# A hybrid recurrent and attention layer: other PSUM slots for the output products, staging slots for the first pair, scans emitted later

## The chip, the cores and the metric

The kernel runs on one core of one Trainium2 chip. The metric is the device time of one execution in microseconds (us). The engines are TensorE (PE, whose weight loads are shown apart as PEld), VectorE (DVE), ScalarE (ACT), GpSimd (POOL) and SyncE (SP), which issues the DMA transfers. Each engine works through its own queue in order and waits on semaphores for the others.

## The reference

One layer of a decoder with two groups of heads side by side, for a prompt of 4096 positions and 8 sampled rows:

```python
def rms_norm(x, g):
    xf = x.astype(jnp.float32)
    y = xf * lax.rsqrt(jnp.mean(xf * xf, axis=-1, keepdims=True) + EPS)
    return (y * g.astype(jnp.float32)).astype(x.dtype)

# per layer (DEPTH = 1), D_MODEL = 1024, SEQ = 4096
# xn = rms_norm(x);  proj = xn @ w_in
#   -> RG-LRU input, its gate, q, k, v, attention gate
# RG-LRU group: causal conv of width 4, then h_t = a_t*h_{t-1} + sqrt(1-a_t^2)*(i_t*x_t)
# attention group: window of 128 keys, 8 query heads, 2 key heads, bias, sinks
# mix = concat(groups * SiLU(gate));  y = x + rms_norm(mix @ w_out)
```

The step that matters here is the last line: a product of 4096 x 1024 activations with the 1024 x 1024 matrix w_out, the norm of each row of the result, and the residual.

## The kernel before

Stage A goes through the positions in 11 chunks (the first of 256 + 8 sampled rows, the others of 384): transpose of the input (prep_A), the recurrent projections (proj_A), the maps of the recurrence (rnn_A) and its scan on VectorE (scan_A). The list A_ORDER at line 32 sets the order in which these are written. Stage B does the projections of the attention group and the attention itself, in units named like 10_1; in its units pT is the transposed probabilities, ph their first half, po the product with V. Both leave their gated results, transposed, in DRAM (mix_d).

Stage C, from line 752, multiplies by w_out. It takes row tiles of 128 in 16 pairs. Numbers are kept as the sum of a coarse part h and a rest l (function parts: ACT makes h, DVE makes l), and a product of two such pairs is three matmuls. Pairs 0 to 2 and 15 go through plain (line 835): two outputs of 512 columns for each row tile (three for the last tile: 512, 256 and 256). Pairs 3 to 14 go through seven (line 872): the pair and w_out are taken as 2 x 2 blocks of 512, and seven products x1 to x7 take the place of eight. One product is 12 matmuls of 512 columns, a pair is 84. ACT copies x1 to u1; DVE makes u2 from x6 and u1, u4 from x5 and u2, adds u4 to x3 and u1 to x2 and so ends the first row tile, makes u3 from x7 and u2, adds u4 to x7 and u3 to x4 and so ends the second. For each row tile ACT makes the squares (squares, line 811) while DVE multiplies by the gain, and finish (line 823) scales by the root and adds the residual, in two operations that read both halves of the row tile in PSUM. Names end in the pair: x7_9, h_9s3 and l_9s3 are of pair 9; finish for the second row tile of pair 6 has the root rs_c6b.

PSUM in stages B and C has these pools: ps_mm, two slots of one bank (512 columns); ps_t and ps_v, one slot of one bank each; ps_s, two slots of two banks each. In seven before, x1, x6 and x5 take turns in ps_mm; x2 and x3 are the two halves of one ps_s tile (x23), x4 and x7 of another (x47); ps_t and ps_v stand empty there but for the 8 sampled rows (function sample_rows, 32 small matmuls, written at pair 4). A slot is handed on when all readers of its tile are done.

The activations of a pair are loaded by load_mix (line 760): two transfers of 512 KB into one tile of tag m, of which there are two slots in turn. The tags hl, hs and long hold the operands h and l; each pair is written out a step ahead of its products. In pairs 0 to 2 prep_T also makes the sums of blocks of w_out that seven needs (wt, th, tl). A scheduler of the framework then sets the order of each engine's queue from the written order, the slots and its estimate of durations, so that the order in the queues is not that of the code.

The pools of the staging area are shared by all stages: tag xf has two slots, used in stage A for the small constants and in the last tile for its output.

Of the kernel before, what the change touches and what calls it, by code (L numbers as in the profile page):

```python
# [9 lines left out]
F32 = mybir.dt.float32  # L10
# [5 lines left out]
P = 128  # L16
# [12 lines left out]

A_ORDER = "P1 L P0 P2 R1 X0 R0 P3 X1 R2 X2 R3 S X3".split()

B_FIRST = "V Q0 K Q1 U00 U01 Q2 Q3 G0 U02 U10 G1 U11 U12 M00 M01 G2 G3 M02 X M10 M11 M12".split()
B_ORDER = "Q0 Q1 K Q2 V U00 U01 Q3 U02 U10 G0 U11 G2 G1 M00 M01 M02 U12 G3 M10 M11 M12 X".split()
# [9 lines left out]
def hymba_kernel(ctx: ExitStack, tc: tile.TileContext, ins, outs):  # L45
    nc = tc.nc
# [12 lines left out]
    NCH = len(chunks)  # L59
# [14 lines left out]
    def ps_mm(n):  # L74
        if phase[0] == "A":
            return ps[0].tile([P, 512], F32, tag="mm", name=n, bufs=4)
        return ps[2].tile([P, 512], F32, tag="mm", name=n, bufs=2)
# [255 lines left out]
    def scan_A(pool, ci, uu, parts):  # L333
        t0, npt, ns = chunks[ci]
        W = npt + ns
        act(uu[:, :, :W], uu[:, :, :W], AF.Sqrt, scale=-0.25)
        for c, (aa, ix, sg) in enumerate(parts):
            nc.vector.tensor_mul(ix, ix, uu[:, c, :W])
            hh = pal.tile([P, STEP], F32, tag="hh", name=f"hh_{ci}_{c}", bufs=4)
            nc.vector.tensor_tensor_scan(hh[:, :npt], aa[:, :npt], ix[:, :npt], hprev[c] if ci else 0.0,  # L340
                                         op0=ALU.mult, op1=ALU.add)
            hprev[c] = const.tile([P, 1], F32, tag=f"hl{c}", name=f"hl_{ci}_{c}", bufs=2)
            nc.gpsimd.tensor_copy(hprev[c], hh[:, npt - 1:npt])
            if ns:
                o = hh[:, npt:W]
                nc.vector.tensor_mul(o, aa[:, npt:W], h0T[:, c, :])
                nc.vector.tensor_add(o, o, ix[:, npt:W])
                nc.gpsimd.tensor_copy(hs[:, c, :], o)
            nc.vector.tensor_mul(hh[:, :W], hh[:, :W], sg[:, :W])
            nc.sync.dma_start(mix_d[ci][:, c, :], hh[:, :W])  # L350
# [76 lines left out]
    st = [{} for _ in chunks]  # L427
    st[0]["x"] = xA
    for ci in range(NCH):
        for item in A_ORDER:  # L430
            f, s = item[0], st[ci]
            c = int(item[1:] or 0)
            if f == "P":
                s["p", c] = proj_A(pa, ci, c, wA, s["x"])
            elif f == "R":
                if "uu" not in s:
                    s["uu"] = pal.tile([P, 4, STEP], F32, tag="uu", name=f"uu_{ci}", bufs=1)
                s["r", c] = rnn_A(pa, ci, c, s["uu"], *s["p", c])
            elif f == "S":
                scan_A(pa, ci, s["uu"], [s["r", c] for c in range(4)])  # L440
            elif ci + 1 < NCH:
                if f == "L":
                    s["n"] = load_A(prep, ci + 1)
                else:
                    x = st[ci + 1].setdefault("x", ([], []))
                    prep_A(ci + 1, s["n"], (2 * c, 2 * c + 1), x)
        if ci == 3:
            setup_bias(pa)
    for c in reversed(cms):
        c.__exit__(None, None, None)  # L450

# [306 lines left out]
    pairs = [rowsC[i:i + 2] for i in range(0, len(rowsC), 2)]  # L758

    def load_mix(pi):  # L760
        m = pcx.tile([P, 2, KD, P], F32, tag="m", name=f"mix_{pi}", bufs=2)
        for j, (ci, off) in enumerate(pairs[pi]):
            nc.sync.dma_start(m[:, j], mix_d[ci][:, :, off:off + P])
        return [[m[:, j, 4 * e:4 * e + 4, :].rearrange("p k c -> p (k c)") for e in range(2)] for j in range(2)]
# [70 lines left out]
    def plain(pi, A):  # L835
        H = [[parts(A[j][e], f"{pi}_{j}{e}", e == 0) for e in range(2)] for j in range(2)]
        for j, (xr, ydst) in enumerate(load_rows(pi)):
            n = f"{pi}_{j}"
            final = pi == len(pairs) - 1 and j == 1
            if final:  # L840
                cuts = [(0, 512), (512, 768), (768, D)]
                po = [f(f"out_{n}_{i}") for i, f in enumerate((ps_mm, ps_t, ps_v))]
            else:
                cuts = [(0, 512), (512, D)]
                if (2 * pi + j) % 3 == 0:
                    po = [ps_mm(f"out_{n}_{i}") for i in range(2)]
                else:
                    po = ps_s(f"out_{n}")
                    po = [po[:, 0:512], po[:, 512:D]]
            po = [p[:, 0:c[1] - c[0]] for p, c in zip(po, cuts)]  # L850
            ss = sums(n)

            def product(e, p, c):
                wh, wl = w_cols(e, c)
                a, b = [t[:, (e % 4) * P:(e % 4 + 1) * P] for t in H[j][e // 4]]
                nc.tensor.matmul(p, a, wh, start=e == 0, stop=False)  # L856
                nc.tensor.matmul(p, a, wl, start=False, stop=False)  # L857
                nc.tensor.matmul(p, b, wh, start=False, stop=e == 7)  # L858

            for e, i in [(e, i) for i in range(3) for e in range(8)] if final else \  # L860
                    [(e, i) for e in range(8) for i in range(2)]:
                product(e, po[i], cuts[i])
            res = []
            for i, (p, c) in enumerate(zip(po, cuts)):
                out = p
                if final and i:
                    out = stage.tile([P, STEP], F32, tag="xf", name=f"pg_{i}", bufs=2)[:, 0:c[1] - c[0]]
                squares(ss, i, p, gpost[:, c[0]:c[1]], n, out)
                res.append((out, c))
            finish(ss, res, xr, ydst, n, final)  # L870

    def seven(pi, A):
        (a11, a12), (a21, a22) = A
        n = f"{pi}"
        p11 = parts(a11, n + "a11", True)
        p22 = parts(a22, n + "a22", where="long")
        nc.vector.scalar_tensor_tensor(a22, a21, 0.5, a22, op0=ALU.mult, op1=ALU.add)
        s1 = parts(a22, n + "s1", where="hs")
        nc.vector.tensor_sub(a21, a11, a21)
        nc.vector.scalar_tensor_tensor(a11, a11, -0.5, a22, op0=ALU.mult, op1=ALU.add)  # L880
        s2 = parts(a11, n + "s2", where="hs")
        p12 = parts(a12, n + "a12")
        nc.vector.tensor_sub(a12, a12, a11)
        s4 = parts(a12, n + "s4", where="hs")
        s3 = parts(a21, n + "s3", True, "hs")
        t1, t2, t3, t4 = [[wT[e][i] for e in range(4)] for i in range(4)]
        lo_c, hi_c = (0, 512), (512, D)
        b11 = [w_cols(e, lo_c) for e in range(4)]
        b21 = [w_cols(4 + e, lo_c) for e in range(4)]
        b22 = [w_cols(4 + e, hi_c) for e in range(4)]  # L890

        (xa, ya), (xb, yb) = load_rows(pi)
        sa, sb = sums(n + "a"), sums(n + "b")
        g0, g1 = gpost[:, 0:512], gpost[:, 512:D]

        def product(out, a, w):
            for k in range(4):
                ah, al = [t[:, k * P:(k + 1) * P] for t in a]
                wh, wl = w[k]
                nc.tensor.matmul(out, ah, wh, start=k == 0, stop=False)  # L900
                nc.tensor.matmul(out, ah, wl, start=False, stop=False)
                nc.tensor.matmul(out, al, wh, start=False, stop=k == 3)

        def keep(m):
            return pc.tile([P, 512], F32, tag="keep", name=f"{m}_{n}", bufs=6)

        x1, x6, x5 = [ps_mm(f"x{i}_{n}") for i in (1, 6, 5)]
        xu, xd = [ps_s(f"x{i}_{n}") for i in (23, 47)]
        x2, x3, x4, x7 = xu[:, lo_c[0]:lo_c[1]], xu[:, hi_c[0]:hi_c[1]], xd[:, lo_c[0]:lo_c[1]], xd[:, hi_c[0]:hi_c[1]]
        product(x1, p11, b11)  # L910
        u1 = keep("u1")
        act(u1, x1, AF.Copy)
        product(x6, s2, t2)
        u2 = keep("u2")
        nc.vector.tensor_add(u2, x6, u1)
        product(x5, s1, t1)
        u4 = keep("u4")
        nc.vector.tensor_add(u4, x5, u2)
        product(x3, s4, b22)
        nc.vector.tensor_add(x3, x3, u4)  # L920
        squares(sa, 1, x3, g1, n + "a")
        product(x2, p12, b21)
        nc.vector.tensor_add(x2, x2, u1)
        squares(sa, 0, x2, g0, n + "a")
        finish(sa, [(x2, lo_c), (x3, hi_c)], xa, ya, n + "a")
        product(x7, s3, t3)
        u3 = keep("u3")
        nc.vector.tensor_add(u3, x7, u2)
        nc.vector.tensor_add(x7, x7, u4)
        squares(sb, 1, x7, g1, n + "b")  # L930
        product(x4, p22, t4)
        nc.vector.tensor_add(x4, x4, u3)
        squares(sb, 0, x4, g0, n + "b")
        finish(sb, [(x4, lo_c), (x7, hi_c)], xb, yb, n + "b")
# [88 lines left out]
```

## Time and profile before

| | before |
|---|---|
| time of the runs, median (lowest to highest) | 1456.89 us (1453.6 to 1457.09) |
| the profiled execution | 1450.32 us |
| its span | 1448.5 us |
| mean granted clock of TensorE | 0.988 |
| busy: PE, DVE, ACT, POOL | 95%, 71%, 57%, 31% |
| stage C | from about 1079 us to the end |

The profiled execution is one run with the profiler; its span is the time from the first to the last instruction. Matmuls overlap, so that the step from one start to the next tells the rate, not the duration in a row. The granted clock is 1.00 at 2.4 GHz and 0.50 at 1.2 GHz; a window between the two has some of each.

### The profile page before, as it was taken

The page shows a single profiled execution, that of the slowest core. Times are in us where ns is not written, and L with a number is a line of the kernel's source. Part 1 is how long each engine was busy: PE and PEld are TensorE (multiplying, and loading weights), DVE is VectorE, ACT ScalarE, POOL GpSimd, SP SyncE. Part 2 cuts the span into 40 slices and gives each one's busy share as a digit, 9 for nine tenths or more (in the row PEclk, how much of TensorE's full clock was granted, in tenths as well). Part 3 has the DMA queues.
Part 4 walks back from the last instruction along what each step waited for, and adds up shares of the span by engine and source line. Part 5 has one row for each costly group of instructions (what it writes and reads, how often), then busy time and mean ns, then how long its engine had stood idle before and what let it go on. Part 6 is the DMA issues. An engine that isn't in the chain of part 4 may idle for free. (4 is left out here: it accounts for less than half of the span.)

```text
span 1448.5 us, 23928 instructions
## 1 busy us (share of the span) xinstructions
PE 1380.2 (95%) x7983; PEld 1298.2 (90%) x7983; DVE 1025.7 (71%) x2421; ACT 831.6 (57%) x2095; POOL 449.6 (31%) x876
## 2 busy tenths in 40 slices
PE   6999999999999799999999999999989998999996
PEld 5999999999999699999999999999988877778775
DVE  6778877777877956656658556566675977777773
ACT  4665656665556757577576676676674433333331
POOL 3323333312321025354353463463452200000000
PEclk9999999999999999999999999999999999999999
DMA  9433354434339132133121220320345544444432
GB/s 274 141 103 124 132 174 143 142 135 149 111 116 262 53 103 95 46 104 99 48 98 39 83 99 13 110 99 12 131 139 173 180 153 133 137 148 143 152 118 102
DMA packets 138982, 174.42 MB, mean 120 GB/s; under 512 B 12615, under 2 KB 120727, under 8 KB 138859
## 3 DMA queue, kind: packets, MB, share of 16 engines
q1 hardware_dynamic: 138858, 172.90, 36.2%
q8 instruction: 63, 1.03, 0.3%
q14 instruction: 61, 0.49, 0.1%
HBM read 104.38 MB, written 68.50 MB: 119 GB/s over the span
## 5 line engine op out<-in xcount | busy, mean ns | idle before, releaser
L124 PE MATMUL pr<-xl,wh_in 128*128 128x384 f32 (+1 forms) x688 | 229.9, 335 | 0.0
L125 PE MATMUL pr<-xh,wl_in 128*128 128x384 f32 (+1 forms) x688 | 228.0, 333 | 0.0
L123 PE MATMUL pr<-xh,wh_in 128*128 128x384 f32 (+1 forms) x688 | 218.2, 337 | 7.9 <-ACT xc L290 7.9
L123 PEld LDWEIGHTS pr<-xh,wh_in 128*128 128x128 f32 x688 | 128.4, 189 | 9.7 <-ACT xc L290 9.4
L603 ACT ACTIVATE tt<-tt,nm 128x129 f32<-128x129 f32 x256 | 99.9, 393 | 61.7 <-DVE nm L600 61.5
L124 PEld LDWEIGHTS pr<-xl,wh_in 128*128 128x128 f32 x688 | 129.7, 189 | 0.7 <-issue 0.7
L125 PEld LDWEIGHTS pr<-xh,wl_in 128*128 128x128 f32 x688 | 129.6, 188 | 0.0
L123 PE MATMUL pga<-xh_B,wh_in 128*128 128x384 f32 (+1 forms) x352 | 119.4, 339 | 0.7 <-ACT qz L547 0.7
L124 PE MATMUL pga<-xl_B,wh_in 128*128 128x384 f32 (+1 forms) x352 | 119.1, 338 | 0.0
L125 PE MATMUL pga<-xh_B,wl_in 128*128 128x384 f32 (+1 forms) x352 | 118.4, 336 | 0.0
L123 PE MATMUL pq<-xh_B,wh_in 128*128 128x384 f32 (+1 forms) x352 | 116.9, 333 | 0.9 <-DVE ksT L507 0.7
L124 PE MATMUL pq<-xl_B,wh_in 128*128 128x384 f32 (+1 forms) x352 | 117.2, 333 | 0.2 <-DMA xl_B<-xT_d 0.2
L125 PE MATMUL pq<-xh_B,wl_in 128*128 128x384 f32 (+1 forms) x352 | 117.1, 333 | 0.0
L292 DVE SCALAR_TENSOR_TENSOR xc<-xr,cT,xc 128x384 f32<-128x384 f32 (+1 forms) x132 | 87.1, 676 | 6.9 <-ACT xc L290 6.5
L630 POOL TENSOR_SCALAR_AFFINE_SELECT p<-ph 64x256 fp32r<-64x256 f32 x124 | 53.4, 431 | 108.5 <-PE po L637 87.5
L123 PEld LDWEIGHTS pga<-xh_B,wh_in 128*128 128x128 f32 x352 | 68.0, 193 | 0.9 <-ACT qz L547 0.9
L652 POOL TENSOR_TENSOR mxb<-mxb,sgb 128x256 f32<-128x256 f32 x64 | 47.2, 743 | 69.3 <-DVE mxb L645 66.0
L124 PEld LDWEIGHTS pga<-xl_B,wh_in 128*128 128x128 f32 x352 | 68.0, 193 | 0.0
L125 PEld LDWEIGHTS pga<-xh_B,wl_in 128*128 128x128 f32 x352 | 67.8, 193 | 0.0
L123 PEld LDWEIGHTS pq<-xh_B,wh_in 128*128 128x128 f32 x352 | 66.1, 188 | 1.4 <-DVE ksT L507 1.0
L616 DVE TENSOR_TENSOR pl<-pT,ph 128x512 fp32r<-128x512 f32 x64 | 44.0, 688 | 32.1 <-PE po L637 23.6
L124 PEld LDWEIGHTS pq<-xl_B,wh_in 128*128 128x128 f32 x352 | 66.1, 188 | 0.7 <-DMA xl_B<-xT_d 0.5
(764 smaller groups left out, 4109.0 us busy)
## 6 DMA issues: line engine op xcount, KB each, us to landing
xs<-in_x_prompt_dram SPq DMA_DIRECT2D x32, 512.0 KB
xr<-in_x_prompt_dram SPq DMA_DIRECT2D x32, 512.0 KB
mix<-mix_d SPq DMA_DIRECT2D x32, 512.0 KB
out_dram<-xr SPq DMA_DIRECT2D x31, 512.0 KB
xT_d<-xh SPq DMA_DIRECT2D x80, 192.0 KB
xT_d<-xl SPq DMA_DIRECT2D x80, 192.0 KB
xh_B<-xT_d SPq DMA_DIRECT2D x80, 192.0 KB
xl_B<-xT_d SPq DMA_DIRECT2D x80, 192.0 KB
```

The costliest lines, as they stand in the source:

```text
L123: nc.tensor.matmul(out, wh, xh, start=first, stop=False)
L124: nc.tensor.matmul(out, wh, xl, start=False, stop=False)
L125: nc.tensor.matmul(out, wl, xh, start=False, stop=last)
L292: nc.vector.scalar_tensor_tensor(xc[:, :npt], xr[:, t:t + npt], cw[:, t, c:c + 1], xc[:, :npt], op0=ALU.mult, op1=ALU.add)
L603: act(tt[:, g, 0:P + 1], tt[:, g, 0:P + 1], AF.Exp, scale=-1.0, bias=nm[:, g:g + 1], accum_out=sm[:, g:g + 1])
L616: nc.vector.tensor_sub(pls, pt, phs)
L630: nc.gpsimd.affine_select(dst, src[r, :, r], pattern=[[0, 4], [-1, HD]], compare_op=ALU.is_gt, fill=0.0, base=0, channel_multiplier=1)
L652: nc.gpsimd.tensor_mul(oo, oo, st["sg", kv][:, :, b * P:(b + 1) * P])
```

## The change

In seven each of the seven products gets a PSUM tile of its own: x1 and then x5 in ps_t, x6 in ps_v, x3 and x2 in the two slots of ps_mm, x7 and x4 in the first 512 columns of one ps_s slot each. The last row tile's first part takes a ps_s slot in place of ps_mm. load_mix for pair 0 fills four tiles of 512 columns of the tag xf, with a transfer of 256 KB each, in place of one tile of tag m. In stage A the scan of a chunk is written behind the first projections (P1) of the next chunk, the last one behind the loop.

```diff
--- before.py
+++ after.py
@@ -29,7 +29,7 @@
 
 
 
-A_ORDER = "P1 L P0 P2 R1 X0 R0 P3 X1 R2 X2 R3 S X3".split()
+A_ORDER = "P1 S L P0 P2 R1 X0 R0 P3 X1 R2 X2 R3 X3".split()
 
 B_FIRST = "V Q0 K Q1 U00 U01 Q2 Q3 G0 U02 U10 G1 U11 U12 M00 M01 G2 G3 M02 X M10 M11 M12".split()
 B_ORDER = "Q0 Q1 K Q2 V U00 U01 Q3 U02 U10 G0 U11 G2 G1 M00 M01 M02 U12 G3 M10 M11 M12 X".split()
@@ -437,7 +437,9 @@
                     s["uu"] = pal.tile([P, 4, STEP], F32, tag="uu", name=f"uu_{ci}", bufs=1)
                 s["r", c] = rnn_A(pa, ci, c, s["uu"], *s["p", c])
             elif f == "S":
-                scan_A(pa, ci, s["uu"], [s["r", c] for c in range(4)])
+                if ci:
+                    s = st[ci - 1]
+                    scan_A(pa, ci - 1, s["uu"], [s["r", c] for c in range(4)])
             elif ci + 1 < NCH:
                 if f == "L":
                     s["n"] = load_A(prep, ci + 1)
@@ -446,6 +448,7 @@
                     prep_A(ci + 1, s["n"], (2 * c, 2 * c + 1), x)
         if ci == 3:
             setup_bias(pa)
+    scan_A(pa, NCH - 1, st[-1]["uu"], [st[-1]["r", c] for c in range(4)])
     for c in reversed(cms):
         c.__exit__(None, None, None)
 
@@ -758,6 +761,14 @@
     pairs = [rowsC[i:i + 2] for i in range(0, len(rowsC), 2)]
 
     def load_mix(pi):
+        if pi == 0:
+
+            out = []
+            for ci, off in pairs[pi]:
+                out.append([stage.tile([P, 512], F32, tag="xf", name=f"mix_0_{len(out)}{e}") for e in range(2)])
+                for e, t in enumerate(out[-1]):
+                    nc.sync.dma_start(t.rearrange("p (k c) -> p k c", c=P), mix_d[ci][:, 4 * e:4 * e + 4, off:off + P])
+            return out
         m = pcx.tile([P, 2, KD, P], F32, tag="m", name=f"mix_{pi}", bufs=2)
         for j, (ci, off) in enumerate(pairs[pi]):
             nc.sync.dma_start(m[:, j], mix_d[ci][:, :, off:off + P])
@@ -839,7 +850,7 @@
             final = pi == len(pairs) - 1 and j == 1
             if final:
                 cuts = [(0, 512), (512, 768), (768, D)]
-                po = [f(f"out_{n}_{i}") for i, f in enumerate((ps_mm, ps_t, ps_v))]
+                po = [f(f"out_{n}_{i}") for i, f in enumerate((ps_s, ps_t, ps_v))]
             else:
                 cuts = [(0, 512), (512, D)]
                 if (2 * pi + j) % 3 == 0:
@@ -904,9 +915,10 @@
         def keep(m):
             return pc.tile([P, 512], F32, tag="keep", name=f"{m}_{n}", bufs=6)
 
-        x1, x6, x5 = [ps_mm(f"x{i}_{n}") for i in (1, 6, 5)]
-        xu, xd = [ps_s(f"x{i}_{n}") for i in (23, 47)]
-        x2, x3, x4, x7 = xu[:, lo_c[0]:lo_c[1]], xu[:, hi_c[0]:hi_c[1]], xd[:, lo_c[0]:lo_c[1]], xd[:, hi_c[0]:hi_c[1]]
+
+        x1, x6, x5 = [f(f"x{i}_{n}") for f, i in ((ps_t, 1), (ps_v, 6), (ps_t, 5))]
+        x3, x2 = [ps_mm(f"x{i}_{n}") for i in (3, 2)]
+        x7, x4 = [ps_s(f"x{i}_{n}")[:, 0:512] for i in (7, 4)]
         product(x1, p11, b11)
         u1 = keep("u1")
         act(u1, x1, AF.Copy)
```

Three places in the queues, before and after. In TensorE's queue at the end of stage B, po is the last attention unit's product with V, out_0_0_0 and out_0_0_1 are the two halves of the first row tile, and h_0_00 is its first operand. Before:

```order
L637 MATMUL po_10_0_2_13331<-ph_10_0_2_13327,vs_10_2_13122 128x4x64
L637 MATMUL po_10_0_2_13331<-pl_10_0_2_13328,vs_10_2_13122 128x4x64
L637 MATMUL po_10_0_2_13331<-p2_10_0_2_13332,vx_10_0_2_13298 128x4x64
L856 MATMUL out_0_0_0_13751<-wh_out0_13680,h_0_00_13731 128x512
L857 MATMUL out_0_0_0_13751<-wl_out0_13681,h_0_00_13731 128x512
L856 MATMUL out_0_0_1_13752<-wh_out0_13680,h_0_00_13731 128x512
L857 MATMUL out_0_0_1_13752<-wl_out0_13681,h_0_00_13731 128x512
L611 MATMUL pT_10_1_1_13478<-ident_101,tt_10_1_1_13461 128x128 x4
L858 MATMUL out_0_0_0_13751<-wh_out0_13680,l_0_00_13732 128x512
```

After (the last two P.V matmuls stand behind the first two of out_0_0_0, and pT_10_1_1 further back):

```order
L640 MATMUL po_10_0_2_13331<-ph_10_0_2_13327,vs_10_2_13122 128x4x64
L867 MATMUL out_0_0_0_13756<-wh_out0_13685,h_0_00_13736 128x512
L868 MATMUL out_0_0_0_13756<-wl_out0_13686,h_0_00_13736 128x512
L640 MATMUL po_10_0_2_13331<-pl_10_0_2_13328,vs_10_2_13122 128x4x64
L640 MATMUL po_10_0_2_13331<-p2_10_0_2_13332,vx_10_0_2_13298 128x4x64
L867 MATMUL out_0_0_1_13757<-wh_out0_13685,h_0_00_13736 128x512
L868 MATMUL out_0_0_1_13757<-wl_out0_13686,h_0_00_13736 128x512
L869 MATMUL out_0_0_0_13756<-wh_out0_13685,l_0_00_13737 128x512
```

In the changed kernel two matmuls of the first tile are ahead of the end of the attention unit.

TensorE's queue at x7 of pair 9. Before, x47_9 of operand h_9s3 is x7_9, and the product ahead of it, x23_9 of operand h_9s4, is x3_9:

```order
L900 MATMUL x23_9_15387<-wh_out7_13722,h_9s4_15370 128x512
L901 MATMUL x23_9_15387<-wl_out7_13723,h_9s4_15370 128x512
L902 MATMUL x23_9_15387<-wh_out7_13722,l_9s4_15371 128x512
L900 MATMUL x47_9_15388<-th_0_2_13896,h_9s3_15374 128x512
L901 MATMUL x47_9_15388<-tl_0_2_13897,h_9s3_15374 128x512
```

After:

```order
L911 MATMUL x2_9_15405<-wh_out7_13727,h_9a12_15382 128x512
L912 MATMUL x2_9_15405<-wl_out7_13728,h_9a12_15382 128x512
L913 MATMUL x2_9_15405<-wh_out7_13727,l_9a12_15383 128x512
L911 MATMUL x7_9_15406<-th_0_2_13901,h_9s3_15391 128x512
L912 MATMUL x7_9_15406<-tl_0_2_13902,h_9s3_15391 128x512
```

x4_8, x3_9 and x7_9 stood in a row before; now x4_8 is the last product of its pair, and x7_9 the sixth of the next, with five products between.

ACT's queue around u1_9, the copy of x1_9; h_11a11 is the first operand of pair 11 and the first reader of its load, sqc the squares. Before:

```order
L770 ACTIVATE h_9s2_15361<-mix_9_15177 128x512
L812 ACTIVATE sqc_8a_1_15278,ssc_8a_15216<-x23_8_15221 128x512
L770 ACTIVATE h_9s4_15370<-mix_9_15177 128x512
L912 ACTIVATE u1_9_15401<-x1_9_15384 128x512
L770 ACTIVATE h_9s3_15374<-mix_9_15177 128x512
L770 ACTIVATE h_11a11_15678<-mix_11_15509 128x512
L812 ACTIVATE sqc_8a_0_15294,ssc_8a_15216<-x23_8_15221 128x512
```

After:

```order
L823 ACTIVATE sqc_8a_0_15311,ssc_8a_15231<-x2_8_15237 128x512
L781 ACTIVATE h_9s3_15391<-mix_9_15192 128x512
L823 ACTIVATE sqc_8b_1_15335,ssc_8b_15232<-x7_8_15238 128x512
L781 ACTIVATE h_10a22_15535<-mix_10_15360 128x512
L823 ACTIVATE sqc_8b_0_15351,ssc_8b_15232<-x4_8_15239 128x512
L781 ACTIVATE h_11a11_15699<-mix_11_15528 128x512
L924 ACTIVATE u1_9_15420<-x1_9_15401 128x512
L781 ACTIVATE h_10s1_15540<-mix_10_15360 128x512
L781 ACTIVATE h_10s2_15546<-mix_10_15360 128x512
```

u1_9 stood two rows ahead of h_11a11 and stands now right behind it.

## Rows read from the trace of the kernel before

**Rows 1.** The page, part 1: busy us of each engine, share, instructions.

```profile
PE 1380.2 (95%) x7983; PEld 1298.2 (90%) x7983; DVE 1025.7 (71%) x2421; ACT 831.6 (57%) x2095; POOL 449.6 (31%) x876
```

**Rows 2.** What TensorE waited for: us in total, times, longest, whole span.

```profile
PE x L900 <- DVE xr L823: 17.8, 5, 4.5
PE pr L123 <- ACT xc L290: 7.9, 6, 2.3
...
PE out L856 <- DVE xr L823: 3.1, 1, 3.1
```

**Rows 3.** Windows: length, busy PE, PEld, DVE, ACT, POOL, granted clock, DMA share, GB/s.

```profile
60.00:90.00 30.00, 27.72 (x164) 27.32 (x163) 23.39 (x54) 19.44 (x33) 12.14 (x20) 1.00 0.39 128
...
1078.00:1080.00 2.00, 0.48 (x1) 0.48 (x2) 1.12 (x2) 1.12 (x3) 1.69 (x4) 0.50 1.17 328
...
1084.00:1086.00 2.00, 2.00 (x9) 1.65 (x8) 0.93 (x2) 0.36 (x1) 0.00 (x0) 0.85 0.61 219
...
1116.00:1152.00 36.00, 36.00 (x160) 29.85 (x159) 34.19 (x61) 19.14 (x40) 5.32 (x3) 1.00 0.66 216
...
1224.00:1260.00 36.00, 32.54 (x139) 26.01 (x138) 28.65 (x49) 12.17 (x26) 2.82 (x4) 0.98 0.45 149
...
1368.00:1404.00 36.00, 32.54 (x147) 26.50 (x146) 26.71 (x45) 12.06 (x27) 1.96 (x3) 1.00 0.38 127
```

**Rows 4.** TensorE matmul by matmul (start, duration) around two x7 products.

```profile
1254.46 0.39 PE L902 MATMUL x<-wh_out,l_7s 128*128 128x512 f32 x1
1258.17 0.47 PE L900 MATMUL x<-th,h_7s 128*128 128x512 f32 x1 [3.32 <-DVE xr L823]
...
1258.73 0.63 PE L902 MATMUL x<-th,l_7s 128*128 128x512 f32 x1
1259.16 0.63 PE L900 MATMUL x<-th,h_7s 128*128 128x512 f32 x1
...
1262.13 0.39 PE L901 MATMUL x<-tl,h_7s 128*128 128x512 f32 x1
1262.36 0.40 PE L902 MATMUL x<-th,l_7s 128*128 128x512 f32 x1
...
1302.11 0.47 PE L900 MATMUL x<-th,h_9s 128*128 128x512 f32 x1 [3.32 <-DVE xr L823]
```

**Rows 5.** VectorE in the same place: start, duration, operation.

```profile
1252.17 0.70 DVE L932 TENSOR_TENSOR x<-x,u 128x512 f32<-128x512 f32 x1 [0.98 <-PE x L902]
...
1256.62 1.40 DVE L823 SCALAR_TENSOR_TENSOR xr<-x,rs_c6b,xr 128x512 f32<-128x512 f32 x2
```

**Rows 6.** Timeline of all engines where stage B ends and C begins.

```profile
1076.45 0.58 ACT L615 ACTIVATE ph<-pT 128x512 fp32r<-128x512 f32 x1
...
1077.44 0.39 PE L637 MATMUL po<-pl,vs 128*128 128x256 f32 x1 [0.21 <-POOL pl L632]
...
1078.84 0.63 ACT L770 ACTIVATE h<-mix 128x512 fp32r<-128x512 f32 x1 [1.81 <-DMA mix<-mix_d]
...
1079.52 0.80 PE L856 MATMUL out<-wh_out,h 128*128 128x512 f32 x1 [1.54 <-ACT h L770]
```

**Rows 7.** SyncE's load of a pair, and ACT's operation that waited for it.

```profile
1132.98 1.24 SPq L763 DMA_DIRECT2D mix<-mix_d  x2
...
1141.00 0.63 ACT L770 ACTIVATE h_4a<-mix 128x512 fp32r<-128x512 f32 x1 [4.26 <-DMA mix<-mix_d]
...
1264.71 1.24 SPq L763 DMA_DIRECT2D mix<-mix_d  x2
...
1269.67 0.63 ACT L770 ACTIVATE h_10a<-mix 128x512 fp32r<-128x512 f32 x1 [1.86 <-DMA mix<-mix_d]
```

**Rows 8.** ACT by line, 1224 to 1400: count, busy us, mean ns.

```profile
L912 ACT ACTIVATE u<-x 128x512 f32<-128x512 f32 x8 | 4.6, 581 | 0.0
```

**Rows 9.** The end of the span: last matmul and the first square behind it.

```profile
1439.88 0.39 PE L858 MATMUL out<-wh_out,l 128*128 128x512 f32 x1
1440.38 0.60 ACT L812 ACTIVATE sqc<-out 128x512 bf16<-128x512 f32 x1 [8.77 <-PE out L858]
```

## The prediction, made before the changed kernel was run

> **What bounds the kernel now.** I began with the busy table: TensorE (PE) is busy for 1380.2 of 1448.5 us [rows 1], so only TensorE's idle or slow time can be won, some 68 us in all. The list of what TensorE waited for, summed by cause, comes next [rows 2]. Its first line is the largest: five waits of 17.8 us together at line 900, all in the output stage. Two more belong to that stage: 3.1 us for the last row tile, and 1.54 us at its first product [rows 6]. The 7.9 us behind ACT's conv rows are in the first stage. The windows of the output stage say what kind of stage it is [rows 3]: without a stop TensorE is busy 36.00 of 36 us (1116 to 1152, with DVE at 34.19), with a stop 32.5, and DVE has then some 28 us of work.
>
> One stop, matmul by matmul [rows 4]: the last matmul of x3 starts at 1254.46, the first of x7 at 1258.17 after 3.32 us idle, released by DVE line 823. The matmuls that follow start 0.43 apart, the lower of the two clock levels, until 1262.13; then 0.23 again. So from 1254.46 to 1262.36, 12 steps that at 0.23 need 2.76 took 7.90: a loss of 5.14, of which 3.32 is the wait and 1.8 the slow clock and the restart. The DVE rows [rows 5] give the reason: x4 of the pair before is read at 1252.17, as soon as TensorE ends it; its square and root follow, and line 823, which reads x4 and x7 for the last time, runs from 1256.62 to 1258.02. x4 and x7 share one two-bank PSUM tile, so x7 of the next pair can't start earlier. At the pairs that stop, TensorE has one product, x3, to do between x4 of the pair before and x7; at the pairs between them it has x1 as well, and doesn't stop.
>
> **The change, part by part.**
>
> *Products.* Every product now has a slot that is freed alone, and the order of TensorE becomes x1, x6, x3, x5, x2, x7, x4 in pairs 3, 4 and 8 to 14. x7 follows x4 of the pair before after five products instead of one, that is 60 x 0.23 = 13.8 us, and line 823 ended 5.85 us after DVE began on x4 (1252.17 to 1258.02). Cover 8 us: the stop goes. Gone are the five waits, 17.8; the slow stretch behind them, 1.8 each, in four of five (the window from 1368 has a stop and a granted clock of 1.00 [rows 3]), 7.2; and the wait of the last row tile, whose first part now takes a slot of the wide pool, 3.1. Smaller waits, under 0.3 each, are left out. Sum 28.1.
>
> *New waits of the single slots.* x5 takes x1's slot, so it waits for ACT's copy u1, 0.58 us [rows 8]; x6 and x3 (5.5 us) lie between, so in step nothing is lost. x1 waits for DVE's u4 from x5 of the pair before: three products between, 8.3 us, against two DVE operations, and nothing is lost. x6 likewise. In pairs 5 to 7 the order is irregular: I walked ACT's order there, and u1 of pair 6 stands behind the squares of pair 5, so x5 of pair 6 is late by about 1.8 and x3 of that pair by 0.7: +2.5. No row shows these waits; the bounds are 0 and, as for the waits they replace, 2 x 5.14.
>
> *The filler.* The 32 sample matmuls stood as filler in pairs 3 to 5, now between pairs 4 and 5. Pair 3 loses it where DVE has least room (34.19 of 36). I charge 1, between 0 and 3.3, one stop's wait.
>
> *The first pair's activations.* At the junction [rows 6] ACT's first h waits for its load and ends its wait at 1078.84, although ACT was free from 1077.03 (its previous operation starts at 1076.45, 0.58 long); TensorE, whose last P.V matmuls start at 1077.44 and just behind, starts at 1079.52. With slots of the staging pool the load of the first half tile is issued hundreds of us earlier, in a gap of the queue in stage A, the second in stage B, so nothing on SP waits for them. h moves ahead of the last P.V's ph, TensorE's first two matmuls between two of its P.V matmuls, at about 1077.1. The price: ph of the last attention unit is 0.6 later, and DVE and POOL behind it; its products have the whole first pair to come in. The other two half tiles wait for staging slots and land at about 1086, and TensorE needs them near 1089. Gain of the start 1.9 (between 0 and 2.4). Then the clock: it was granted at 0.50 from 1078 [rows 3], and TensorE was back at full rate only near 1086, so of 5 us about half is lost, 2.4. Whether it still falls can't be read: 2.3 us of idle in stage A [rows 2] left the clock at 1.00 there [rows 3], 3.32 brought it down. I take half, 1.2, between 0 and 2.4.
>
> *The scans.* In the order of the two kernels nothing moves in stages A and B on TensorE, ACT, DVE or POOL; only the two loads go in on SP. Worth 0.
>
> *The end.* The last product is now the 256-column piece, with the squares of the wide one done before. From the last matmul to the end of the span were 8.6 us (1439.88 to 1448.5) [rows 9]; one square of 512 columns, 0.60, and its read less: -0.8 (0 to 1.5).
>
> Sum: 28.1 + 3.1 + 0.8 - 2.5 - 1 = 28.5. The profiled execution took 1450.32, so 1421.8. The runs' median is 6.57 above the profiled one: **1428.4**, rounded 1428.
>
> **The rivals.**
>
> *A. The load loop sets the pair's length.* Here I found least room. In the new ACT order u1 of pair n stands behind h_a11 of pair n+2, which waits for that pair's load; before, it stood ahead of it. The load is issued when DVE has made the last operand of pair n, l_s3, which in DVE's order follows u3 and x7 of pair n-1. From the end of x7 of pair n-1 to x5 of pair n lie four products, 48 x 0.23 = 11.0 us. In them: three to six DVE operations of 0.70 [rows 5], 2.1 to 4.2; the load, 4.96 from issue to h in the usual case, 8.02 in the worst [rows 7]; h 0.63 [rows 7] and u1 0.58 [rows 8]. That is 8.3 to 10.4, so it fits by 0.6 to 2.7. With a load 2 us longer than usual behind a full DVE, each of nine pairs is 1.4 longer, and the clock doesn't fall for so short a stop: +12.6, 1441. For it: DVE has 28.65 us of work in 36 (1224 to 1260 [rows 3]) at a period of 43.9 for two pairs (the stops at x7 of pairs 7 and 9 end at 1258.17 and 1302.11 [rows 4]), so 17.5 in a pair of 19.3, and the pairs now follow each other faster. Against it: the usual load.
>
> *B. The stop only moves.* Half of the gain comes back elsewhere, because DVE's in-order queue makes another slot or operand late: +14, 1442. For it: the window of 1116 with DVE at 34.19. Against it: DVE's 17.5 fit into 19.3.
>
> *C. A stop at every product: slower.* With one slot for each product, TensorE asks a semaphore of ACT or DVE 84 times; if each answer comes as late as the small wait at the junction, 0.21 [rows 6], that is 17.6 us. If besides the clock falls once in each of 12 pairs, 1.8 each, 21.6 more: 1428.4 + 39.2 = 1468. It is slower than before from 28.5 us, that is 2.4 us in each pair. Against it: in the windows without a stop TensorE changes products at 36.00 busy and clock 1.00 [rows 3], with the pools of before.
> The Trainium skill, "TensorE: Matmul & The Clock Gate", section "A second HAM failure mode: psum-queue depth-cycling", speaks for C: cycling through PSUM banks makes TensorE idle briefly between groups of matmuls so often that its clock goes down and up. By it the time would be that of C; the window from 1116 does not agree, with six banks in use and a clock of 1.00.
>
> *D. The change does not do what it says.* For the scans that is so, and counted. For the products it would be so if x7 still waited for line 823; cover of 8 us speaks against it. Then 1450.
>
> **How the numbers follow.** Forecast 0.60, A 0.24, B 0.07, D 0.04, C 0.05. The range: the bounds of the unknown terms put the forecast between 1419 and 1437 (junction +1.7 or -3.1, new waits +2.5 or -7.8, filler +1 or -2.3, seldom all together), and A reaches 1443. Below 1418 and above 1443 I leave some 2 in 10. A difference under 0.3%, 4.4 us, can't be told from none here. Faster by more: forecast, A and B, 0.91; within: D, 0.04; slower: C, 0.05.
>
> **What the new profile would show.** Right: no wait of TensorE for line 823 in the stage's list, windows from 1188 on at 35.5 or more of 36 and clock 1.00, nine pairs 19.3 us long. A: x5 waiting for ACT's u1, ACT's h for the load, once a pair. B: a new line for h or l operands. C: a short idle ahead of each product and a clock below 1. Junction: first out matmul within 0.5 us of the last P.V. Wrong would be the forecast if pairs 8 to 14 were longer than 20.5 us.

## The result and the profile after

The changed kernel took 1419.51 us in the median (1416.61 to 1424.18, four runs) against 1456.99 beside it: a ratio of 0.9749, 95% interval 0.9717 to 0.978. Beside other runs of the kernel before, on other occasions, it took 1419.59 (ratio 0.9765, 0.9738 to 0.9792) and 1420.02 (0.9771, 0.9747 to 0.9795). The profiled execution took 1416.61, its span is 1414.5: 33.9 less than before.

The page of the changed kernel, part 1, answers to [rows 1]: TensorE is busy for 13.4 us less, although it does the same matmuls, since a matmul at the low clock is busy for longer (0.63 us against 0.39 in [rows 4]).

```profile
PE 1366.8 (97%) x7983; PEld 1290.1 (91%) x7983; DVE 1023.1 (72%) x2421; ACT 829.9 (59%) x2095; POOL 445.0 (31%) x876
```

What TensorE waited for from 1070 to the end, all but one line of 0.2, answers to [rows 2] (us in total, times, longest):

```profile
PE po L640 <- POOL pl L635: 1.7, 1, 1.7
PE x L911 <- ACT u L924: 1.4, 2, 1.2
PE x L911 <- ACT h_7s L781: 0.5, 1, 0.5
```

No wait for a finish (line 834 here) is left. The waits that came are two for u1 and one for an h of pair 7. The windows answer to [rows 3], with the same columns:

```profile
1080.00:1084.00 4.00, 4.00 (x19) 3.30 (x18) 1.46 (x3) 1.82 (x6) 3.60 (x8) 1.00 1.19 298
1116.00:1152.00 36.00, 36.00 (x161) 29.80 (x160) 32.82 (x60) 19.72 (x41) 7.04 (x3) 1.00 0.60 195
...
1188.00:1224.00 36.00, 34.28 (x150) 26.13 (x149) 28.35 (x49) 13.05 (x28) 2.82 (x4) 1.00 0.38 120
1224.00:1260.00 36.00, 36.00 (x160) 29.81 (x159) 31.50 (x54) 14.59 (x31) 2.50 (x4) 1.00 0.57 188
...
1332.00:1368.00 36.00, 36.00 (x161) 29.80 (x160) 31.03 (x54) 13.80 (x29) 2.19 (x4) 1.00 0.52 157
```

From 1080 to 1404 TensorE is busy for all of 36 us but in two windows, 35.82 in that from 1152 and 34.28 in that from 1188, where pairs 5 to 7 lie. For the latter the prediction had named 35.5 or more as a sign: that sign was missed, by the waits of pairs 6 and 7. The granted clock is 1.00 in every window from 1080 to 1404, and VectorE has 31.5 us of work in 36 (1224 to 1260) where it had 28.65.

At x7 of pair 9, matmul by matmul (start, duration), which answers to [rows 4]:

```profile
1284.71 0.39 PE L912 MATMUL x<-wl_out,h_9a 128*128 128x512 f32 x1
1284.94 0.39 PE L913 MATMUL x<-wh_out,l_9a 128*128 128x512 f32 x1
1285.16 0.39 PE L911 MATMUL x<-th,h_9s 128*128 128x512 f32 x1
1285.39 0.39 PE L912 MATMUL x<-tl,h_9s 128*128 128x512 f32 x1
```

x2 ends, x7 begins in step, 0.22 later. The finish of the pair before, in VectorE's rows, which answers to [rows 5]:

```profile
1272.77 0.69 DVE L944 TENSOR_TENSOR x<-x,u 128x512 f32<-128x512 f32 x1
...
1277.11 1.40 DVE L834 SCALAR_TENSOR_TENSOR xr<-x,rs_c8b,xr 128x512 f32<-128x512 f32 x2
```

It runs from 1277.11 to 1278.51, where x4 was read at 1272.77; x7 starts 6.65 us behind its end. A pair lasts 19.04 us (x1 of pairs 8 and 9 start at 1252.52 and 1271.56), where two lasted 43.9.

The junction, all engines, answers to [rows 6]:

```profile
119.76 0.37 SPq L770 DMA_DIRECT2D mix<-mix_d  x1
...
1077.50 0.62 ACT L781 ACTIVATE h<-mix 128x512 fp32r<-128x512 f32 x1
...
1077.67 0.39 PE L640 MATMUL po<-pl,vx 128*128 128x256 f32 x1 [1.71 <-POOL pl L635]
...
1078.17 0.50 PE L867 MATMUL out<-wh_out,h 128*128 128x512 f32 x1
...
1078.74 0.28 PE L640 MATMUL po<-pl,vs 128*128 128x256 f32 x1
```

The first matmul of the output stage stands between two P.V matmuls, and h, at 1077.50, waits for no load: line 770, the load of the first half tile, was issued at 119.76.

### The profile page after: what moved, and what is told of

The parts are those of the page before. It is cut to its first block, busy times and chain, and to the rows that moved or that the text cites. A ratio compares the mean times of both kernels' runs of the same rounds, so it can differ in the third digit from the quotient of the medians.

```text
span 1414.5 us, 23962 instructions
## 1 busy us (share of the span) xinstructions
PE 1366.8 (97%) x7983; PEld 1290.1 (91%) x7983; DVE 1023.1 (72%) x2421; ACT 829.9 (59%) x2095; POOL 445.0 (31%) x876
## 5 line engine op out<-in xcount | busy, mean ns | idle before, releaser
L321 ACT ACTIVATE thr<-gt,hba 128x384 f32<-128x384 f32 (+1 forms) x44 | 25.2, 573 | 72.3 <-PE gt L125 71.4
L125 PEld LDWEIGHTS pq<-xh_B,wl_in 128*128 128x128 f32 x352 | 66.9, 190 | 0.3 <-issue 0.2
```

The lines of the kernel that those rows point to most:

```text
L125: nc.tensor.matmul(out, wl, xh, start=False, stop=last)
L321: act(thr, pg[:, 0:W], AF.Tanh, scale=0.5, bias=hba[:, c:c + 1])
```

## The experiments

Each kernel below was profiled, and timed where a ratio is given.

**The PSUM slots alone** (the kernel before with the new slots of seven and of the last tile).

```diff
-        x1, x6, x5 = [ps_mm(f"x{i}_{n}") for i in (1, 6, 5)]
-        xu, xd = [ps_s(f"x{i}_{n}") for i in (23, 47)]
...
+        x1, x6, x5 = [f(f"x{i}_{n}") for f, i in ((ps_t, 1), (ps_v, 6), (ps_t, 5))]
+        x3, x2 = [ps_mm(f"x{i}_{n}") for i in (3, 2)]
+        x7, x4 = [ps_s(f"x{i}_{n}")[:, 0:512] for i in (7, 4)]
```

> The kernel before with the PSUM slots of the change alone (products and the last tile). Theory (the shared x4/x7 tile was the cause, the parts add up): the five waits for the second row tile's finish and the slow clock behind them go, the start of the output stage stays as before; the profiled run 28 to 31 us shorter than 1450.3, so 1419 to 1422, ratio 0.978 to 0.981; clock 0.50 again from 1078 to 1084. Rival (the first pair's staging opens the way, the slots alone gain little because VectorE is full early in the stage): under 20 us, with new waits in pairs 2 to 4.

Measured: 1421.9 us against 1452.7, ratio 0.9778 (0.9758 to 0.9798); span 1416.5, 32.0 less. What TensorE waited for in stage C (us in total, times, longest):

```profile
PE x L900 <- ACT u L912: 1.2, 1, 1.2
PE out L856 <- ACT h L770: 1.1, 1, 1.1
PE x L900 <- ACT h_7s L770: 0.5, 1, 0.5
```

The waits for the finish are gone, and the start still waits for h, 1.1; the clock fell there too, to 0.62 from 1080 to 1084. The profiled run, 1418.33, is 0.7 shorter than the shortest that I expected. So the slots alone bring nearly all of the gain: the time of the whole change is 0.9749 to 0.9771 of that before, and the intervals overlap with this one.

**The first pair's staging alone.**

```diff
+        if pi == 0:
+
+            out = []
+            for ci, off in pairs[pi]:
+                out.append([stage.tile([P, 512], F32, tag="xf", name=f"mix_0_{len(out)}{e}") for e in range(2)])
...
```

> The kernel before with the first pair's activations in staging slots alone. Theory: the output stage starts 1.3 us earlier relative to the attention's end and the clock does not fall there (2.4), the five waits stay 17.8 long; 2 to 4 us gained if pairs 0 to 5 pass it on, ratio 0.997 to 0.999. Rival: the gain is lost at the first wait for a finish (VectorE sets its time), 0 to 1 us.

Measured: 1452.47 against 1452.7, ratio 0.9993 (0.9982 to 1.0004), so at most 2.6 us gained. From the last matmul of the last gate projection to the first of stage C it took 3.58 us (1076.07 to 1079.65), before 6.00: the start is earlier by 2.4, where I had expected 1.3. But the finish still stops x7:

```profile
PE x L908 <- DVE xr L831: 18.2, 6, 4.5
PE out L864 <- DVE xr L831: 3.1, 1, 3.1
```

and the clock fell at the junction all the same (the window's columns are those of [rows 3]):

```profile
1080.00:1084.00 4.00, 4.00 (x13) 3.16 (x12) 2.93 (x6) 3.20 (x10) 2.86 (x7) 0.58 1.07 294
```

The second part of the expectation, that the clock is kept, fell. The interval also admits the rival's 0 to 1 us.

**The scans alone.**

```diff
-A_ORDER = "P1 L P0 P2 R1 X0 R0 P3 X1 R2 X2 R3 S X3".split()
+A_ORDER = "P1 S L P0 P2 R1 X0 R0 P3 X1 R2 X2 R3 X3".split()
...
+    scan_A(pa, NCH - 1, st[-1]["uu"], [st[-1]["r", c] for c in range(4)])
```

> The kernel before with the scans written behind the next chunk's first projections alone. Theory: the queues of TensorE, ScalarE, VectorE and GpSimd are the same, so 0, ratio within 0.998 to 1.002. Rival (the timed gain of the whole change, 37.5, is larger than that of the profiled runs, 33.7, because the scans gain what the order does not show): 2 to 4 us, ratio 0.997 to 0.9985.

Measured: 1454.17 against 1452.7, ratio 1.0009 (0.9997 to 1.0021). Nothing, as the queues said.

**x4 and x7 in one wide tile again**, all else as changed.

```diff
-        x7, x4 = [ps_s(f"x{i}_{n}")[:, 0:512] for i in (7, 4)]
+        xd = ps_s(f"x47_{n}")
+        x4, x7 = xd[:, lo_c[0]:lo_c[1]], xd[:, hi_c[0]:hi_c[1]]
```

> The changed kernel with x4 and x7 again as halves of one wide tile, all other slots as changed (the wide pool has two slots, so x7 of the next pair takes the other one). Theory (x7 waited because its slot was the one that the finish of the pair before still read): no wait for a finish of the pair before, time within 5 us of the changed kernel, 1415 to 1425. Rival (a tile of its own for each product is what counts): the waits for line 834 (finish) come back at x7, 10 us or more above the changed kernel.

Measured: 1425.05, ratio 0.98 (0.9781 to 0.9819), some 5 us above the changed kernel. No wait for a finish came back:

```profile
PE x L911 <- ACT h_6s L781: 2.6, 1, 2.6
PE x L911 <- ACT u L925: 1.8, 4, 1.1
```

So a tile for each product is not needed. With x2 and x3 out of the wide pool, the tiles x47 of two pairs take its two slots in turn, and that is enough: all but one matmul of x7 of pair 9 run ahead of x4 of pair 8 (h_8a below), and so long before the finish of pair 8.

```profile
1284.71 0.39 PE L912 MATMUL x<-tl,h_9s 128*128 128x512 f32 x1
1284.93 0.39 PE L911 MATMUL x<-th,h_8a 128*128 128x512 f32 x1
...
1292.31 1.40 DVE L834 SCALAR_TENSOR_TENSOR xr<-x,rs_c8b,xr 128x512 f32<-128x512 f32 x2
```

**Both wide tiles again**, x1, x5 and x6 in the single slots as changed.

```diff
-        x3, x2 = [ps_mm(f"x{i}_{n}") for i in (3, 2)]
-        x7, x4 = [ps_s(f"x{i}_{n}")[:, 0:512] for i in (7, 4)]
+        xu, xd = [ps_s(f"x{i}_{n}") for i in (23, 47)]
+        x2, x3, x4, x7 = xu[:, lo_c[0]:lo_c[1]], xu[:, hi_c[0]:hi_c[1]], xd[:, lo_c[0]:lo_c[1]], xd[:, hi_c[0]:hi_c[1]]
```

> The changed kernel with the two wide tiles back (x2 and x3 halves of one, x4 and x7 of the other); x1, x5 and x6 stay in the single-slot pools, staging and scans stay. Theory (x7 stops because both wide slots are taken in every pair, so that its slot is the one the finish of the pair before reads): the queue has x3 and x7 close behind x4 again, stops of 3 to 4.5 us at x7 in most of pairs 5 to 13 and the slow clock behind them: 1440 to 1450, ratio 0.991 to 0.998. Rival (x1, x5 and x6 off the two-slot pool were the cause): within 5 us of the changed kernel.

Measured: 1463.22 against 1454.67, ratio 1.0061 (1.0036 to 1.0085): slower than before, outside what I expected. The waits came back, as more and shorter ones:

```profile
PE x L911 <- DVE x L824: 13.5, 8, 3.3
PE x L911 <- DVE xr L834: 10.8, 10, 3.9
```

Ten are for the finish, seven of them of some 0.5 us at x7 of pairs 6 to 12, where I had expected 3 to 4.5. Eight, the larger sum, are at x4 of pairs 4 to 11 for the product with the gain in the other half of the same wide tile, which I had not foreseen. Two of them, at x4 of pair 6 and x7 of pair 7:

```profile
1257.67 0.50 PE L911 MATMUL x<-th,h_6a 128*128 128x512 f32 x1 [1.29 <-DVE x L824]
...
1266.65 0.50 PE L911 MATMUL x<-th,h_7s 128*128 128x512 f32 x1 [0.52 <-DVE xr L834]
```

In stage C the idle time is 24.8 us, before 21.5 (the sum of the idle times ahead of its matmuls); the end is long besides: the last matmul starts at 1441.80, and the last tile's residual is loaded only when a row slot comes free, so that line 834 waits for it until 1453.51:

```profile
1441.80 0.39 PE L869 MATMUL out<-wh_out,l 128*128 128x512 f32 x1
...
1453.51 0.75 DVE L834 SCALAR_TENSOR_TENSOR xr<-out,rs_c,xr 128x512 f32<-128x512 f32 x1 [4.07 <-DMA xr<-in_x_prompt_dram]
```

**Other homes for the seven tiles**: x1, x6, x5 in the two-slot pool, x3 and x2 in the single slots, x7 and x4 as changed.

```diff
-        x1, x6, x5 = [f(f"x{i}_{n}") for f, i in ((ps_t, 1), (ps_v, 6), (ps_t, 5))]
-        x3, x2 = [ps_mm(f"x{i}_{n}") for i in (3, 2)]
+        x1, x6, x5 = [ps_mm(f"x{i}_{n}") for i in (1, 6, 5)]
+        x3, x2 = [f(f"x{i}_{n}") for f, i in ((ps_t, 3), (ps_v, 2))]
```

> The changed kernel with other homes for the same seven tiles: x1, x6, x5 in turn in the two-slot pool as before, x3 and x2 in the single-slot pools, x7 and x4 in the wide pool. Theory (what counts is that x7's and x4's slots are freed alone, which pools the others use is nothing): within 3 us of the changed kernel, no wait for a finish. Rival (x1, x6, x5 in the single slots are what spaces the products): waits come back at x5 or x3, 5 us or more longer.

Measured: 1417.41, ratio 0.9751 (0.9724 to 0.9778); no wait for a finish, one of 0.9 for u1. Once more, with more rounds:

> The kernel with x1, x6, x5 in the two-slot pool and x3, x2 in the single slots once more, beside the changed kernel. Theory: it has no wait for u1 in pairs 6 and 7 (1.7 us less), so 0 to 3 us below the changed kernel, at the edge of what can be told.

Measured: 1418.23, ratio 0.9751 (0.9729 to 0.9774), where the changed kernel beside it had 0.9771; the intervals overlap, so it can't be called faster. Its list for stage C has one wait of TensorE other than POOL's:

```profile
PE x L911 <- ACT u L924: 0.5, 1, 0.5
```

**A later load**: one, then two small transfers ahead of the first half of each load from pair 8 on, which the load waits for.

```diff
+            for _ in range(1 if j == 0 and pi >= 8 else 0):
+                nc.sync.dma_start(m[:, j, 0:1], mix_d[ci][:, 0:1, off:off + P])
             nc.sync.dma_start(m[:, j], mix_d[ci][:, :, off:off + P])
```

> The changed kernel with one more small transfer (64 KB) ahead of the first half of each pair's load from pair 8 on, for which the load itself waits. In the changed kernel u1 was done 3.4 us before x5 asked for it (pair 9: 1276.35 to 1279.7), so rival A's loop has 3.4 us of room. Theory: the load lands some 2.3 us later, TensorE waits for nothing, span within 2 us of the changed kernel's 1414.5. Rival (the loop is tight): each of 7 pairs 1 to 2 us longer, 7 to 14 us.

Measured (one run): 1419.19, span 1417.5, within the 1414.5 to 1418.0 of the changed kernel's three profiles. TensorE waits for nothing in pairs 8 to 14, although ACT's first h of pair 11 comes 8.6 us behind the small transfer (1275.26 to 1283.89), where it came 4.3 behind the load.

> The same with two such transfers one after the other: the load some 4.6 us later, 1.2 beyond the room of 3.4. Theory: TensorE waits for u1 at x5 (or x3) in about 7 pairs, 1 to 1.5 us each, span 7 to 12 us above the changed kernel's. Rival (the load's place in ScalarE's queue doesn't matter): no wait, span unchanged.

Measured (one run): 1430.51, span 1428.8, 10.8 to 14.3 above the changed kernel's spans. What TensorE waited for from 1240 to 1400, three lines:

```profile
PE x L913 <- ACT u L926: 5.5, 5, 1.2
PE x L913 <- ACT sqc_12b L825: 1.2, 1, 1.2
PE x L913 <- ACT sqc_11b L825: 1.2, 1, 1.2
```

Pairs 11 and 12 are 22.2 us apart (the stops at x3 end at 1318.30 and 1340.50). But these two don't settle rival A as it was put: in both the scheduler, which saw the longer load, placed u1 ahead of the waiting h in ACT's queue, where the changed kernel has it behind. A kernel with that queue unchanged and the load later was not run; that part stays open.

**The last tile's first part in the two-slot pool again.**

```diff
-                po = [f(f"out_{n}_{i}") for i, f in enumerate((ps_s, ps_t, ps_v))]
+                po = [f(f"out_{n}_{i}") for i, f in enumerate((ps_mm, ps_t, ps_v))]
```

> The changed kernel with the last tile's first part in the two-slot pool again. Theory: with the pairs' own slots that pool's reader is done early, so no wait of 3 us; but the 512-column part is last in TensorE's queue, so three squares follow the last matmul in place of one: end of span 1 to 1.5 us later. Rival (the wide slot is what removed the 3.1 us wait): a wait of some 3 us at line 867 and 4 us longer.

Measured (one run): 1420.58, span 1418.9. There is no wait at line 867. The 512-column part is last in TensorE's queue; behind its last matmul, at 1410.71, ACT does three squares:

```profile
1411.22 0.60 ACT L823 ACTIVATE sqc<-out 128x512 bf16<-128x512 f32 x1 [8.45 <-PE out L869]
...
1411.94 0.38 ACT L823 ACTIVATE sqc<-out 128x256 bf16<-128x256 f32 x1
...
1412.44 0.38 ACT L823 ACTIVATE sqc<-out 128x256 bf16<-128x256 f32 x1
...
1414.98 1.31 SPq L836 DMA_DIRECT2D out_dram<-xr  x3
```

From there to the end it took 8.15 us, in the changed kernel 6.76: 1.4 more, within the 1 to 1.5 expected.

**The changed kernel twice more.**

> The changed kernel once more, timed beside the kernel before and profiled again. Theory: 33 to 38 us shorter than before, ratio 0.974 to 0.978. Open is the clock where the output stage starts: in the first profile it stayed at 1.00 there; the two other kernels with the same staging (alone, and with x4 and x7 in one tile) showed 0.50 from 1080 to 1084. If the staging keeps the clock up, it is 1.00 again; if it is where the fall happens to lie, it may be 0.50 here and the span then some 2 us longer.

> The changed kernel beside it: 33 to 36 us below the kernel before, ratio 0.975 to 0.978. The clock where the output stage starts: 1.00 if the first out matmul starts before 1078.3, a fall to 0.50 if it starts after 1079, as in the seven profiles with this staging so far.

Measured: 1419.59 and 1420.02, the ratios given above; spans 1414.6 and 1418.0. The window of the start of stage C, in the first of them and in the last:

```profile
1080.00:1084.00 4.00, 4.00 (x21) 3.33 (x21) 0.00 (x0) 0.71 (x2) 2.10 (x5) 1.00 1.17 292
```

```profile
1080.00:1084.00 4.00, 4.00 (x13) 3.17 (x12) 2.69 (x5) 2.96 (x9) 3.11 (x7) 0.57 1.17 312
```

## Why the prediction was right, and where its sizes were off

The forecast was 1428 us with a range of 1418 to 1443; measured were 1419.5 to 1420.0. Against its own profiled execution it was 1421.8, measured 1416.6. That the waits for the finish go, and with them some 30 us, held; the gain was larger than the sum, and the time lies only 1.5 us inside the range.

*The sum and the range.* To come from the profiled execution to the median I had added 6.57; in the changed kernel the two differ by 2.9 alone. Beside later runs the kernel before had medians of 1452.7 to 1454.7, not 1456.9, so that some 2 to 4 of the 6.57 look like a chance of the three runs that I had. This is 3.7 of the 8.9 us by which 1428.4 was too high; the other 5.2 are gone through below. The lower end of 1419 that I gave for the forecast does not follow from its terms, which add up to no less than 1423.2 (1422.5 with the end); that 1419.5 lies inside is luck in part. And the 68 us of the first paragraph are idle time alone: what slow matmuls cost stands in the busy time, of which 13.4 us went.

*Products (28.1).* Right, if small. The excess of stage C, the steps of its matmuls above 0.2265 us for 512 columns (0.1175 for 256), sums to 35.0 us before and 3.9 after; of these 21.5 and 1.9 are idle time, 7.5 and 0 are steps at the low clock, 6.0 and 2.0 the restarts. So 19.6 of idle and 11.5 of slow clock and restarts went, the clock of the junction among them. Of the cover of 8 us 6.65 were there.

*Why the finish stops x7.* The wait was the right one, the reason given for it was right in part. I had named the shared tile of x4 and x7; with that tile back and x2, x3 elsewhere no stop came, with both wide tiles back the stops came. Where both slots of the wide pool are taken in every pair, x7 gets, by the code, the slot that the finish of the pair before reads last. But that is so in the changed kernel too, where x7 and x4 take one each, and it doesn't stop. What differs there is the order: five products stand between x4 and the next x7, where one stood before at the pairs that stopped, and two with both wide tiles from pair 6 on, so that x7 starts 6.65 us behind the end of the finish. A stop needs both, a slot that is read late and a queue that asks for it early. The shared tile is not harmless either: with both wide tiles x4 waited 13.5 us for VectorE's work in x7's half. How much the order gains without the new slots no run shows, nor why the scheduler chose it.

*New waits (+2.5).* The place was right, the size 1.9: x5 of pair 6 waited 1.23 for u1, behind the four squares of pair 5, the last two of which stand in ACT's rows,

```profile
1217.02 0.60 ACT L823 ACTIVATE sqc_5b<-x 128x512 bf16<-128x512 f32 x1
...
1217.74 0.60 ACT L823 ACTIVATE sqc_5b<-x 128x512 bf16<-128x512 f32 x1
...
1218.32 0.59 ACT L924 ACTIVATE u<-x 128x512 f32<-128x512 f32 x1
```

but x3 did not wait, and x6 of pair 7 waited 0.49 for its operand instead; 0.18 more at pair 4.

*The filler (+1).* 0: pair 3 had no stop in the first profile, 0.18 in the second. *The last tile (3.1).* The wait went, but the wide slot that I gave as the reason is not needed for it: it is gone too when that part stays in the two-slot pool and comes last in the queue. *The end (-0.8).* 1.8 (8.60 from the last matmul's start to the end of the span, now 6.76): I had counted one square less, but two more of 256 columns stood behind it. The rows that answer to [rows 9]:

```profile
1407.78 0.28 PE L869 MATMUL out<-wh_out,l 128*128 128x256 f32 x1
1408.15 0.38 ACT L823 ACTIVATE sqc<-out 128x256 bf16<-128x256 f32 x1 [2.40 <-PE out L869]
...
1410.65 1.31 SPq L836 DMA_DIRECT2D out_dram<-xr  x3
```

*The junction (3.1).* The start: 2.4 (6.00 to 3.58 from the last gate projection), I had 1.9. The clock: all of it, 1.00, in the first profile, and a fall in the third; half was a fair value for a thing that goes either way, and that the first profile had all of it was luck. Against this stages A and B ended 1.07 later in the first profile; over the profiles of kernels with the same queues there (before and after) that end varies by 3 us.

Together: the end 1.0, the clock 1.2, the start 0.5, the new waits 0.6, the filler 1, and the small waits and restarts that I had left out, some 2, less the 1.07. That is 5.2 us, by which the profiled run was shorter than forecast; the small waits and restarts are what the other terms leave of stage C.

*Rival A* did not come. The load took 4.26 to 4.81 us in pairs 9 to 15, and the loop had more room than my 0.6 to 2.7: in ACT's rows h of pair 11 ends its wait at 1275.23 and u1 of pair 9 runs until 1276.35,

```profile
1275.23 0.63 ACT L781 ACTIVATE h_11a<-mix 128x512 fp32r<-128x512 f32 x1 [1.00 <-DMA mix<-mix_d]
1275.77 0.58 ACT L924 ACTIVATE u<-x 128x512 f32<-128x512 f32 x1
```

and x5 asks for it at 1279.72, 3.4 us later:

```profile
1279.72 0.39 PE L911 MATMUL x<-th,h_9s 128*128 128x512 f32 x1
```

*Rivals B and D* did not come. *C* did not either: 36.00 of 36 busy at a clock of 1.00 with a tile for each product. What the Trainium skill, "TensorE: Matmul & The Clock Gate", section "A second HAM failure mode: psum-queue depth-cycling", tells of another kernel is not borne out here: this one goes through six banks in each of pairs 8 to 14 without a stop. *The scans* brought nothing, as told.

## What to carry to other kernels

Ask of each PSUM slot which reader is its last and how many products stand between that and the next writer. A pool whose slots are all taken in every round gives the next round a slot that this round's slowest reader may still hold, however many banks lie empty beside it; whether it stops depends on how much work is queued in between (here one product was too few, two stopped for 0.5 us in one kernel, five were enough). Two products in one tile can besides wait for each other's readers. A stop of 3.32 us on TensorE cost here half as much again, in slow steps behind it, in three cases of four. And staging one load earlier gave at most 2.6 us alone; on top of the slots the runs can't tell its gain from none.

## What was not expected of the hardware

The fall of the clock at the start of stage C doesn't go with the idle time ahead of it. In all eleven profiles with this staging TensorE was idle there for 1.95 to 1.97 us, in two pieces. Four of them showed a clock of 1.00: the changed kernel twice (first matmul of the stage at 1078.17 and 1076.40), the load later by two transfers (1077.05) and both wide tiles (1080.97). Seven had a fall to 0.50. Six of these began the stage from 1078.98 to 1079.89, among them the third profile of the changed kernel (1079.40) and the staging alone (1079.65). The seventh, the second profile with other homes for the tiles, began it earliest of all, at 1076.09, and its row has the columns of [rows 3]:

```profile
1078.00:1080.00 2.00, 2.00 (x6) 1.61 (x5) 1.38 (x3) 1.74 (x6) 1.74 (x5) 0.50 1.16 327
```

So the start of the third profile of the changed kernel fits what I expected of it, but an early start doesn't keep the clock up, and the length of the idle time doesn't decide. What does, these runs don't show.
